# Moving conditioning blocks of an attention stage from TensorE to VectorE, GpSimd and ScalarE

## The chip, the cores and the metric

The kernel runs on one core of a Trainium2 chip. The metric is the device time of one execution in microseconds. The kernel before was run three times; the median is 1000.45 us. One further execution was recorded by the hardware profiler, and all profile lines come from it.

The core has five engines, each with a queue that it works through in order: TensorE (PE: matrix products and transposes), VectorE (DVE), ScalarE (ACT), GpSimd (POOL) and SyncE (SP, which here only issues DMA transfers). PEld is the loading of weights into TensorE, which overlaps its products.

## The reference

One step of a two-layer model over 128 context tokens and 256 latent tokens, with 1024 features. All arithmetic is float32. What matters here:

```python
def adaln(cond, w_ada, b_ada):                     # one conditioning vector per group
    mod = silu(cond) @ w_ada + b_ada               # 1024 -> 6 * 1024
    return split(mod, 6)                           # shift, scale, gate; twice
def modulate(h, shift, scale): return h * (1 + scale) + shift

for l in range(2):
    sm, cm, gm, sf, cf, gf = adaln(c, w_ada[l], b_ada[l])
    h = modulate(rmsnorm(x), sm, cm)
    mix = attention(h) if l == 0 else gmlp(h)
    x = x + gm * mix
    h = modulate(rmsnorm(x), sf, cf)
    x = x + gf * conv_ffn(h)
```

There are two conditionings, `c_ctx` for the context tokens and `c` for the latent tokens, so every modulation vector is computed for two input vectors with the same weights. In attention (layer 0) the latent queries see a window of their 4 x 64 grid, with a learned bias per head and offset, and 128 cached context keys in the same softmax; the context tokens attend to each other. There are 16 heads of 64 features.

## The kernel before, in words

Features lie on the 128 partitions and the 384 tokens on the columns. A weight is loaded as float32 into a tile `st`, rounded by ScalarE into `hi` and completed by VectorE with `lo = st - hi`; each product is then three products (`mac`, lines 112 to 114). These weight units (128 x 1024, 512 KB) come through a pool of three `st` tiles. In attention, `ready()` splits the oldest one and asks SP for another, `products()` uses one for the queries or the keys of one head pair.

The attention loop runs over eight head pairs. In a cycle of pair t, TensorE computes the scores of query block 0 (`scores(0)`, with those of the context queries), turns the first softmax of pair t-1 (`turn`), computes the products for the keys of t+1, the scores of query block 1, turns the second softmax of t-1, computes the products for the queries of t+1, and then the values of t-1 (`values`). On the other engines `exps` adds the bias (VectorE, line 636, with a minimum beside it) and takes exponentials with sums (ScalarE, line 646), `normalized` divides (VectorE, 651 and 653), `turned` copies the turned softmax from PSUM (ScalarE, 668 and 669; its result `pT` feeds `values`), `keys` and `queries` split into high and low parts (`khi`, `klo`, `qhi`, `qlo`). `bias(btr)` (line 619) writes the bias of the next pair into `bt`, from rows that SP has loaded into `btr` and a mask, by VectorE.

The conditioning is spread over the kernel in blocks of 512 KB. It is computed in two ways. `Ada` (lines 174 to 222) is TensorE's: a block is 128 rows of weights for 1024 outputs, four products of 128 x 256 with the two conditionings as stationary operand (line 199), accumulated over eight blocks; `flush` then turns the result with two transposes (line 215) and adds the bias (line 217). In attention it works off 16 blocks, of the second shift `SF` and the second scale `CF` of layer 0: two ahead of the loop and two at the end of each of the first seven cycles. `AdaV` (lines 226 to 271) is VectorE's: a block is the transposed weight of 128 outputs, `half(c, ...)` multiplies it with conditioning c, broadcast to all partitions (`cs[c]`), and sums over the columns in one instruction (line 260); after the second half the bias is added (line 263). In attention it works off eight blocks of the gate `GM`, one half after `exps(0)` and the other late in the cycle.

Blocks of `Ada` have a ring of two tiles (`adw`), blocks of `AdaV` in attention another of two (`adb`).

The program text is the order of work: for TensorE, ScalarE, VectorE and SP every instruction stands in its engine's queue in the order in which the code issues it. A load waits on SP until its tile is free, and all later loads wait behind it. GpSimd, in attention, only issues the output of the context keys (line 588) and of the values.

Of the kernel before, what the change touches and what calls it, by code (L numbers as in the profile page):

```python
# [11 lines left out]
AF = mybir.ActivationFunctionType  # L12
ALU = mybir.AluOpType
# [10 lines left out]
NPAIR = 8  # L24
# [6 lines left out]
SM, CM, GM, SF, CF, GF = range(6)  # L31
# [8 lines left out]
def backbone(ctx: ExitStack, tc: tile.TileContext, x_in, cond_in, condr_in, b_ada_in, prm_in,  # L40
# [17 lines left out]
    def bank(pool):  # L58
        return pool.tile([P, 512], F32, name="bank", tag="bank")
# [70 lines left out]

    def ada_tile(ring):

        tag = ("adw", "adb")[ring % 2]
        return adp.tile([P, D], F32, name=tag, tag=tag)

    def ada_load(f, late=False):

        w = []
        for hf in range(2):
            st = ada_tile(hf)  # L140
# [31 lines left out]
    class Ada:  # L172
# [3 lines left out]
        def __init__(self):  # L176
            order = [(0, SF), (0, CF)]
            self.todo = [(l, pc, k) for l, pc in order for k in range(KD)]
            self.ready = []
            self.pa = self.done = None  # L180

        def load(self, n):
            for _ in range(n):
                if len(self.ready) == ADA_BUFS or not self.todo:
                    return
                l, pc, k = self.todo.pop(0)
                t = ada_tile(0)
                nc.sync.dma_start(t, w_ada[k * P:(k + 1) * P, (pc - GM) * D:(pc - GM + 1) * D])
                self.ready.append((l, pc, k, t))
# [37 lines left out]
    class AdaV:  # L227


        def __init__(self):  # L230
            self.cs = self.junk = None

            def both(l, p, q):
                return [(l, pc, k) for k in range(KD) for pc in (p, q)]

            def one(l, p):
                return [(l, p, k) for k in range(KD)]

# [12 lines left out]

        def load(self, ring):
            l, pc, k = self.todo.pop(0)
            t = ada_tile(ring)
            nc.sync.dma_start(t, w_adaT[l, pc, k])
            return l, pc, k, t

        def half(self, c, l, pc, k, t):
            m = mods[l][:, pc, k]
            tc.keep_in_program_order(nc.vector.tensor_tensor_reduce(  # L260
                self.junk, t, self.cs[c], 1.0, 0.0, ALU.mult, ALU.add, m[:, c:c + 1]))
            if c:
                nc.vector.tensor_scalar(m, m, b_ada[:, l, pc * 8 + k:pc * 8 + k + 1], None, ALU.add)
                if pc in (CM, CF):
                    gain(l, pc, slice(k, k + 1))

        def run(self, n):
            for _ in range(n):
                block = self.load(len(self.todo))
                for c in range(2):  # L270
                    self.half(c, *block)
# [134 lines left out]
    def attention(pool, wkp):  # L406
# [208 lines left out]
        def bias(btr):  # L615
            for hh in range(2):
                v = btr[:, hh]
                slots = bass.AP(v.tensor, v.offset, [v.ap[0], (62, 3), (31, 2), (1, 64)])
                nc.vector.tensor_tensor(
                    bt[:, hh, 0::2].rearrange("p g (j c) -> p g j c", j=2),  # L620
# [90 lines left out]
        kT, btr = cache(1), bias_load(1)  # L711
        ada.run(2)
        ada.load(2)
        old = None
        for t in range(NPAIR):
# [5 lines left out]
            e = exps(0, sc, pr, pc)  # L721
            ada_v.half(0, *blocks[0])
            if old is not None:
# [41 lines left out]

        output(0, range(6), ps_mm)
        pT.append(turned(1, turn(*old[1])))
        normalized(*e)
# [5 lines left out]
        ready()  # L774
        ada_v.half(1, *blocks.pop(0))
        pT = [turned(0, turn(pr[0], pc[0]))]
# [263 lines left out]
```

## Time and profile before

| | us |
|---|---|
| median of three runs | 1000.45 (999.57 to 1000.53) |
| the profiled execution | 1000.85 |
| its span, first to last instruction | 998.0 |
| TensorE busy | 982.9 |
| VectorE busy | 797.4 |
| ScalarE busy | 476.3 |
| GpSimd busy | 15.8 |
| line 199 (conditioning on TensorE), busy | 8.6 |

Line 619 is the bias; line 260 the conditioning on VectorE. The loop's cycles begin at 67.2, 79.2, 95.4, 110.0, 124.9, 139.5, 154.2 and 168.8 us of the span; attention ends near 210. A line of a profile's group has the source line, the engine, the operation, output <- inputs, shapes, the count, busy time and mean duration of one in ns, and the idle time of that engine just before with what ended it. A line of the order of time has start and duration in us (of a merged run, where several instructions follow each other), engine and source line, the operation, and in brackets the idle time before it. A row of stretches has, for each engine, busy us and the number of instructions, then the granted TensorE clock, the DMA share and GB/s.

### The profile page before, as it was taken

The page shows a single profiled execution, that of the slowest core. Times are in us where ns is not written, and L with a number is a line of the kernel's source. Part 1 is how long each engine was busy: PE and PEld are TensorE (multiplying, and loading weights), DVE is VectorE, ACT ScalarE, POOL GpSimd, SP SyncE. Part 2 cuts the span into 40 slices and gives each one's busy share as a digit, 9 for nine tenths or more (in the row PEclk, how much of TensorE's full clock was granted, in tenths as well). Part 3 has the DMA queues.
Part 4 walks back from the last instruction along what each step waited for, and adds up shares of the span by engine and source line. Part 5 has one row for each costly group of instructions (what it writes and reads, how often), then busy time and mean ns, then how long its engine had stood idle before and what let it go on. Part 6 is the DMA issues. An engine that isn't in the chain of part 4 may idle for free.

```text
span 998.0 us, 15825 instructions
## 1 busy us (share of the span) xinstructions
PE 982.9 (98%) x5942; PEld 934.9 (94%) x5942; DVE 797.4 (80%) x1652; ACT 476.3 (48%) x846; POOL 15.8 (2%) x31
## 2 busy tenths in 40 slices
PE   8999999999999999999999999999999999999996
PEld 5788888899999999999988899999999999999996
DVE  5668888689998889899899999687698777777552
ACT  4455656558554544333363334333485444443331
POOL 1000000000000000000000000000000000000000
PEclk9999999999999999999999999999999999999999
DMA  9886676442464445677737756465235333435521
GB/s 338 313 292 179 206 233 201 138 148 85 148 190 152 167 148 156 201 220 220 235 105 256 251 174 185 149 204 177 84 106 182 122 126 121 127 114 180 161 72 63
DMA packets 53019, 172.94 MB, mean 173 GB/s; under 512 B 6016, under 2 KB 11152, under 8 KB 52944
## 3 DMA queue, kind: packets, MB, share of 16 engines
q1 hardware_dynamic: 51840, 169.33, 53.2%
q10 hardware_dynamic: 576, 1.31, 0.3%
q0 software_dynamic: 528, 1.32, 0.3%
q8 instruction: 46, 0.75, 0.3%
q14 instruction: 29, 0.24, 0.1%
HBM read 169.31 MB, written 2.62 MB: 172 GB/s over the span
## 4 chain that ended last, share of the span: by engine, by line
PE 94%; DVE 2%; ACT 1%; issue 1%; POOL 1%; DMA 1%; POOLq 0%; SPq 0%; ACTq 0%
PE bank L113 29%; PE bank L114 29%; PE bank L112 29%; PE bank L678 1%; PE bank L629 1%; PE bank L912 1%; PE bank L661 1%; PE bank L155 1%; PE bank L199 1%; POOL ry L331 1%; DMA lo<-in_x 1%; PE bank L322 0%; DVE lo L118 0%; PE bank L303 0%; DVE bank L636 0%
## 5 line engine op out<-in xcount | busy, mean ns | idle before, releaser
L113 PE MATMUL bank<-hlo,hi 128*128 128x384 f32 (+1 forms) x976 | 330.5, 339 | 0.1
L112 PE MATMUL bank<-hhi,hi 128*128 128x384 f32 (+1 forms) x976 | 330.1, 338 | 0.0
L114 PE MATMUL bank<-hhi,lo 128*128 128x384 f32 (+1 forms) x976 | 329.9, 338 | 0.2 <-DVE lo L118 0.2
L105 ACT CAST hi<-st 128x1024 fp32r<-128x1024 f32 (+1 forms) x184 | 189.1, 1030 | 295.3 <-PE bank L113 237.9
L106 DVE TENSOR_TENSOR lo<-st,hi 128x1024 fp32r<-128x1024 f32 (+1 forms) x184 | 220.5, 1198 | 62.5 <-ACT hi L105 62.3
L114 PEld LDWEIGHTS bank<-hhi,lo 128*128 128x128 f32 x976 | 184.1, 189 | 0.7 <-DVE lo L118 0.5
L112 PEld LDWEIGHTS bank<-hhi,hi 128*128 128x128 f32 x976 | 184.0, 189 | 0.8 <-ACT hi L105 0.4
L113 PEld LDWEIGHTS bank<-hlo,hi 128*128 128x128 f32 x976 | 183.4, 188 | 0.6 <-DVE hlo L118 0.3
L114 PE MATMUL bank<-ahi,lo 128*128 128x384 f32 x352 | 118.3, 336 | 0.0
L113 PE MATMUL bank<-alo,hi 128*128 128x384 f32 x352 | 118.3, 336 | 0.0
L112 PE MATMUL bank<-ahi,hi 128*128 128x384 f32 x352 | 118.1, 336 | 0.0
L260 DVE CUSTOM_DVE_ANT_0 junk<-adb,cs 128x1024 bf16<-128x1024 f32 x72 | 87.8, 1219 | 0.5
L260 DVE CUSTOM_DVE_ANT_0 junk<-adw,cs 128x1024 bf16<-128x1024 f32 x56 | 68.3, 1220 | 0.5
L114 PEld LDWEIGHTS bank<-ahi,lo 128*128 128x128 f32 x352 | 66.2, 188 | 0.0
L113 PEld LDWEIGHTS bank<-alo,hi 128*128 128x128 f32 x352 | 66.2, 188 | 0.0
L112 PEld LDWEIGHTS bank<-ahi,hi 128*128 128x128 f32 x352 | 66.2, 188 | 0.0
L112 PE MATMUL bank<-hi,hhi 128*128 128x512 f32 x144 | 58.1, 404 | 0.4 <-ACT hhi L453 0.4
L113 PE MATMUL bank<-lo,hhi 128*128 128x512 f32 x144 | 56.9, 395 | 0.1
L114 PE MATMUL bank<-hi,hlo 128*128 128x512 f32 x144 | 56.7, 394 | 0.0
L394 DVE SCALAR_TENSOR_TENSOR x<-bank,mod,x 128x128 f32<-128x128 f32 x64 | 23.8, 413 | 33.1 <-PE bank L114 33.0
L113 PE MATMUL bank<-mlo,hi 128*128 128x384 f32 x128 | 43.6, 341 | 0.0
L112 PE MATMUL bank<-mhi,hi 128*128 128x384 f32 x128 | 43.3, 338 | 0.0
(180 smaller groups left out, 1299.8 us busy)
## 6 DMA issues: line engine op xcount, KB each, us to landing
st<-in_w_up SPq DMA_DIRECT2D x88, 512.0 KB, 3.6
adb<-in_w_adaT SPq DMA_DIRECT2D x36, 512.0 KB, 4.5
st<-in_w_down SPq DMA_DIRECT2D x32, 512.0 KB, 3.6
adw<-in_w_adaT SPq DMA_DIRECT2D x28, 512.0 KB, 3.6
adw<-in_w_ada SPq DMA_DIRECT2D x24, 512.0 KB, 5.8
st<-in_w_qk SPq DMA_DIRECT2D x16, 512.0 KB, 4.2
st<-in_w_gu SPq DMA_DIRECT2D x16, 512.0 KB, 4.4
st<-in_w_gv SPq DMA_DIRECT2D x16, 512.0 KB, 4.4
```

Of the source, the lines that this page charges most:

```text
L105: nc.scalar.copy(hi[:, :n], st[:, :n])
L106: nc.vector.tensor_tensor(lo[:, :n], st[:, :n], hi[:, :n].bitcast(F32), ALU.subtract)
L112: nc.tensor.matmul(out, a[0], b[0], start=start, stop=False)
L113: nc.tensor.matmul(out, a[0], b[1], start=False, stop=False)
L114: nc.tensor.matmul(out, a[1], b[0], start=False, stop=stop)
L155: nc.tensor.matmul(pa[32 * j:32 * j + 32, 0:P], cond_s[:, 4 * hf + kk, :], w[hf][:, kk, P * q:P * q + P], start=(kk == 0), stop=(kk == 3), ...
L199: nc.tensor.matmul(self.pa[32 * j:32 * j + 32, 0:256], cond_s[:, k, :], t[:, 256 * j:256 * j + 256], start=(k == 0), stop=(k == KD - 1), t ...
L260: tc.keep_in_program_order(nc.vector.tensor_tensor_reduce(self.junk, t, self.cs[c], 1.0, 0.0, ALU.mult, ALU.add, m[:, c:c + 1]))
L331: nc.gpsimd.tensor_tensor(y, v, mhalf[:, :n], ALU.pow)
L394: nc.vector.scalar_tensor_tensor(x[m][:, a:b], ps[:, a:b], mod(l, gate, m, c), x[m][:, a:b], ALU.mult, ALU.add)
L629: nc.tensor.matmul(sc[hh][:, cols], q[qp][HS[hh], qs:qs + P], k[kp][HS[hh], ks], start=i == 0, stop=i == 2)
L661: nc.tensor.transpose((ta[:, o:o + P] if g < 2 else tb[:, o - 512:o - 512 + P]), pr[:, b, g * P:g * P + P], ident)
```

## The change

- `Ada` in attention does only the second scale `CF`: eight blocks, one ahead of the loop, one at the end of each of seven cycles and one behind the loop.
- `AdaV` does the gate `GM` and the shift `SF`, alternating: 16 blocks in attention, two in each cycle (A and B). For all but the last block, VectorE takes conditioning 0 as before (`half(0, ...)`), GpSimd multiplies the block in place with conditioning 1 (`shared`), ScalarE sums the product with a copy that has an accumulator (`summed`), and VectorE adds the bias (`biased`). A's sum stands behind the second `exps` of its cycle, B's in the next cycle, behind the split of a weight unit. The last block's two halves stay with VectorE, behind the loop.
- `bias(btr)` is computed by GpSimd.
- All blocks share one ring of four tiles (`adw` and `adb` in turn).
- In the first cycle the queries are split ahead of the next weight unit, in the others behind it.

```diff
-    def ada_tile(ring):
-        tag = ("adw", "adb")[ring % 2]
+    ada_count = iter(range(1 << 20))
+    def ada_tile():
+        tag = ("adw", "adb")[next(ada_count) % 2]
...
-            order = [(0, SF), (0, CF)]
+            order = [(0, CF)]
...
-            self.todo = (one(0, GM) + both(1, SM, CM)[:8]
+            self.todo = (both(0, GM, SF) + both(1, SM, CM)[:8]
...
             if c:
-                nc.vector.tensor_scalar(m, m, b_ada[:, l, pc * 8 + k:pc * 8 + k + 1], None, ALU.add)
-                if pc in (CM, CF):
-                    gain(l, pc, slice(k, k + 1))
+                self.biased(l, pc, k)
+
+        def biased(self, l, pc, k):
+            m = mods[l][:, pc, k]
+            nc.vector.tensor_scalar(m, m, b_ada[:, l, pc * 8 + k:pc * 8 + k + 1], None, ALU.add)
+            if pc in (CM, CF):
+                gain(l, pc, slice(k, k + 1))
+
+        def shared(self, l, pc, k, t):
+            self.half(0, l, pc, k, t)
+            nc.gpsimd.tensor_tensor(t, t, self.cs[1], ALU.mult)
+
+        def summed(self, l, pc, k, t):
+            nc.scalar.activation(t, t, AF.Copy, accum_out=mods[l][:, pc, k, 1:2])
...
-                nc.vector.tensor_tensor(
+                nc.gpsimd.tensor_tensor(
                     bt[:, hh, 0::2].rearrange("p g (j c) -> p g j c", j=2),
...
-        ada.load(2)
-        blocks = [ada_v.load(1) for _ in range(2)]
+        A, B = ada_v.load(), ada_v.load()
+        ada.load(1)
+        A2 = ada_v.load()
...
-        ada.run(2)
-        ada.load(2)
-        old = None
+        old = B1 = None
         for t in range(NPAIR):
...
             e = exps(0, sc, pr, pc)
-            ada_v.half(0, *blocks[0])
+            ada_v.shared(*A)
...
             ready()
+            if B1 is not None:
+                ada_v.summed(*B1)
+                ada.load(1)
+                if not last:
+                    A2 = ada_v.load()
...
             e = exps(1, sc, pr, pc)
+            ada_v.summed(*A)
             if last:
                 break
             if old is not None:
                 pT.append(turned(1, turn(*old[1])))
             bias(btr)
+            ada_v.shared(*B)
             normalized(*e)
-            ada_v.half(1, *blocks.pop(0))
+            if B1 is not None:
+                ada_v.biased(*B1[:3])
+            ada_v.biased(*A[:3])
+            B2 = ada_v.load()
             p = products()
-            ready()
-            Q = queries(p)
+            if old is not None:
+                ready()
+                Q = queries(p)
+            else:
+                Q = queries(p)
+                ready()
...
-            ada.run(2)
-            ada.load(2)
-            if t < NPAIR - 2:
-                blocks.append(ada_v.load(1))
+            ada.run(1)
+            A, B1, B = A2, B, B2
...
         output(0, range(6), ps_mm)
+        ada.run(1)
...
-        ada_v.half(1, *blocks.pop(0))
+        for blk in (B1, A):
+            ada_v.biased(*blk[:3])
+        for c in range(2):
+            ada_v.half(c, *B)
```

More of the change, by code (lines that the diff above doesn't have):

```diff
@@ L139, in ada_load @@
         for hf in range(2):
-            st = ada_tile(hf)
+            st = ada_tile()
             if late:
@@ L186, in load @@
                 l, pc, k = self.todo.pop(0)
-                t = ada_tile(0)
+                t = ada_tile()
                 nc.sync.dma_start(t, w_ada[k * P:(k + 1) * P, (pc - GM) * D:(pc - GM + 1) * D])
@@ L250, in silu, with load @@
                 nc.scalar.activation(self.cs[c], self.cs[c], AF.Silu)
-        def load(self, ring):
+        def load(self):
             l, pc, k = self.todo.pop(0)
-            t = ada_tile(ring)
+            t = ada_tile()
             nc.sync.dma_start(t, w_adaT[l, pc, k])
@@ L262, in half @@
             if c:
-                nc.vector.tensor_scalar(m, m, b_ada[:, l, pc * 8 + k:pc * 8 + k + 1], None, ALU.add)
-                if pc in (CM, CF):
-                    gain(l, pc, slice(k, k + 1))
+                self.biased(l, pc, k)
[9 more added lines that the diff above has]
+            nc.scalar.activation(t, t, AF.Copy, accum_out=mods[l][:, pc, k, 1:2])
         def run(self, n):
             for _ in range(n):
-                block = self.load(len(self.todo))
+                block = self.load()
                 for c in range(2):
```

## The prediction

> **What bounds the kernel now.** I read the page's busy shares and chain first, then the stretch of one cycle of the attention loop (one head pair, from the scores of query block 0 to those of the next pair), then that cycle in order of time on each engine.
>
> ```profile
> span 998.0 us, 15825 instructions
> PE 982.9 (98%) x5942; PEld 934.9 (94%) x5942; DVE 797.4 (80%) x1652; ACT 476.3 (48%) x846; POOL 15.8 (2%) x31
> PE 94%; DVE 2%; ACT 1%; issue 1%; POOL 1%; DMA 1%; POOLq 0%; SPq 0%; ACTq 0%
> 95.40:110.00 14.60, 14.60 (x116) 12.62 (x112) 12.13 (x33) 8.64 (x24) 0.54 (x1) 1.00 0.67 205
> ```
>
> TensorE is busy 98% of the span and for all 14.60 us of a cycle; VectorE is busy 12.13 of them, ScalarE 8.64, GpSimd 0.54. So what leaves TensorE here is worth its time, as long as the other engines go on delivering. How late they may be stands in the order of time. TensorE:
>
> ```profile
> 109.04 1.07 PE L199 MATMUL bank<-adw,cond_s 128*32 128x256 f32 x16
> 110.04 0.44 PE L629 MATMUL bank<-khi,qhi 64*128 64x384 f32 x2
> 121.91 0.38 PE L215 MATMUL bank<-ident,ada_sb 128*128 128x128 f32 x2
> 122.22 0.65 PE L678 MATMUL bank<-pT,V 128*64 128x256 f32 x4
> 154.15 0.44 PE L629 MATMUL bank<-khi,qhi 64*128 64x384 f32 x2
> 169.24 0.34 PE L629 MATMUL bank<-khi,qlo 64*128 64x384 f32 x2
> ```
>
> Two conditioning blocks (L199) hold TensorE from 109.04 to 110.04: 0.50 us a block. Without the two transposes of a finished chunk (L215, once), the values (L678) would have begun at 121.91. The first scores that read qlo come 15.09 us after the cycle's start (154.15 to 169.24); for the cycle from 110.04 that is 125.13. VectorE and ScalarE in that cycle:
>
> ```profile
> 112.55 1.21 DVE L260 CUSTOM_DVE_ANT_0 junk<-adb,cs 128x1024 bf16<-128x1024 f32 x1
> 114.64 0.75 DVE L653 TENSOR_SCALAR pr<-pr,st 128x384 f32<-128x384 f32 x2
> 115.31 0.47 DVE L653 TENSOR_SCALAR pc<-pc,st 128x128 f32<-128x128 f32 x2
> 116.23 1.23 DVE L118 TENSOR_TENSOR lo<-st,hi 128x1024 fp32r<-128x1024 f32 x1 [0.45 <-ACT hi L117]
> 118.53 0.56 DVE L636 CUSTOM_DVE_ANT_0 bank<-bank,bt 128x384 f32<-128x384 f32 x1
> 119.18 0.58 ACT L646 ACTIVATE pr<-bank,st 128x384 f32<-128x384 f32 x1 [0.27 <-DVE st L636]
> 119.52 1.02 DVE L619 TENSOR_TENSOR bt<-mask,btr 128x384 f32<-128x384 f32 x2
> 120.31 0.59 ACT L668 COPY pT<-bank 128x512 f32<-128x512 f32 x1
> 120.65 0.75 DVE L653 TENSOR_SCALAR pr<-pr,st 128x384 f32<-128x384 f32 x2
> 120.77 0.51 ACT L669 COPY pT<-bank 128x384 f32<-128x384 f32 x1
> 121.14 1.08 ACT L117 CAST hi<-st 128x1024 fp32r<-128x1024 f32 x1
> 121.32 1.22 DVE L260 CUSTOM_DVE_ANT_0 junk<-adb,cs 128x1024 bf16<-128x1024 f32 x1
> 122.58 0.23 DVE L263 TENSOR_SCALAR mod<-mod,b_ada 128x2 f32<-128x2 f32 x1
> 122.72 1.22 DVE L118 TENSOR_TENSOR lo<-st,hi 128x1024 fp32r<-128x1024 f32 x1
> 123.85 0.55 DVE L595 SCALAR_TENSOR_TENSOR qlo<-bank,qhi 128x384 fp32r<-128x384 f32 x1
> ```
>
> The second pT is copied by 121.28 and wanted at 121.91: 0.63 us of slack. qlo is done at 124.40 and wanted at 125.13: 0.73 us. Both slacks are short, and everything that the change adds to ScalarE and GpSimd stands ahead of these two.
>
> **The change, part by part.**
>
> *TensorE.* Eight of 16 blocks leave, and the two transposes of one chunk. Each of the seven cycles loses one block: 7 x 0.50 = 3.5 us at most. Of the last, one block is moved from ahead of the loop to behind it, which I count as nothing. The transposes were 0.31 us in front of the values, and the cycle with them is about 0.2 longer: -0.2.
>
> *ScalarE.* Each cycle gets two sums over 128x1024 with an accumulator. The nearest row is the square of x with the same shape and accumulator:
>
> ```profile
> 7.19 1.06 ACT L477 ACTIVATE hi<-lo 128x1024 f32<-128x1024 f32 x1 [0.47 <-DMA lo<-in_x]
> 8.25 0.20 ACT L481 ACTIVATE cond_s<-cond 128x16 f32<-128x16 f32 x1
> ```
>
> From one start to the next is 1.06 us. The old B's sum stands behind the first cast of a weight unit and before the keys; ScalarE has gaps there (it waits at 119.18), and by the order of the casts I estimate that exps(1) moves by 0.2. A's sum stands between exps(1) and the pT copies, with no gap: the copies, the next cast, its lo and qlo all move by 1.06.
>
> *VectorE.* Per cycle it still has two reductions of 1.2 us (the other conditioning's half moves to another block, not away); it loses the bias subtraction (1.02) and gains one 0.23 addition. That is a gain of 0.8 in busy time, but lo then waits for ScalarE's cast, not for VectorE.
>
> *GpSimd.* It gets a 128x1024 product of two SBUF tiles twice a cycle and two 128x384 subtractions. No row shows such an instruction. The nearest, and a clash:
>
> ```profile
> 3.63 0.32 POOL masks.py:199 TENSOR_SCALAR_AFFINE_SELECT ident<-ident 128x128 f32<-128x128 f32 x1
> 9.80 0.24 DVE L334 SCALAR_TENSOR_TENSOR rt<-rt,rv 128x3 f32<-128x3 f32 x1
> 9.81 0.53 POOL L415 TENSOR_SCALAR_AFFINE_SELECT mask<-mask 64x48 f32<-64x48 f32 x2
> 10.08 0.16 DVE L336 SCALAR_TENSOR_TENSOR rr<-rt,ry 128x3 f32<-128x3 f32 x1
> 219.32 1.23 DVE L106 TENSOR_TENSOR lo<-st,hi 128x1024 fp32r<-128x1024 f32 x1
> 219.56 1.74 POOL L331 TENSOR_TENSOR ry<-rv,mhalf 128x3 f32<-128x3 f32 x1 [55.70 <-DVE rv L329]
> 495.58 0.85 POOL L331 TENSOR_TENSOR ry<-rv,mhalf 128x3 f32<-128x3 f32 x1 [274.29 <-DVE rv L329]
> ```
>
> A select over 128 columns takes 0.32, one over 48 about 0.24 (0.53 for two, lapping): 1.1 ns a column and 0.18 fixed, with one operand read. If a second operand costs nothing, the product is 0.18 + 1024 x 1.1 ns = 1.3 us and a subtraction 0.6; if it costs as much as the first, 2.4 and 1.0. I take the upper ends, because the product has two full operands to fetch. [...]
>
> GpSimd's 128x3 power takes 0.85 at 495.58, with VectorE idle, and 1.74 at 219.56, under VectorE's lo, which ends at 220.55: it looks as if it began only then. In the other direction, L334, which has tiny operands, took 0.24 beside the first select where its like L336 took 0.16. So the two engines block each other, and I let whoever asks first hold the other off to its end. [...]
>
> Through one cycle, with lo, the reductions and the normalization (whose 384 columns cost only 0.14 more than 128: 0.47 and 0.75 for two) exposed:
> - Reduction of A ends at 113.8. GpSimd's product holds 113.9 to 116.3. Normalization, due at 114.64 and 1.14 long, runs 116.3 to 117.4; lo starts at 117.4, not 116.23. exps(1) is 1.2 late: VectorE is done with it at 120.8, ScalarE at 121.5.
> - ScalarE: sum 1.06, copies 0.97, cast 1.0: pT at 123.5, the cast at 124.5. TensorE begins the values at 123.6, 1.7 later than 121.91.
> - VectorE: reduction of B 120.8 to 122.0; GpSimd's first subtraction, which asked in between, to 123.0; normalization to 123.8; second subtraction to 124.8; lo 124.8 to 126.0; qlo to 126.5. The qlo scores start at 126.6, against 125.13: **+1.47 us**. (By TensorE's own line, 123.6 + 1.67 + 0.5 + 0.45 = 126.2.)
> - B's product, asked for at 124.8, comes behind lo, at 126.0, and ends before A's next reduction.
>
> Six cycles have this shape (pairs 1 to 6): 6 x 1.47 = +8.8. Pair 0 has no copies of pT, and its queries are moved ahead of a lo:
>
> ```profile
> 81.10 0.45 PE L629 MATMUL bank<-khi,qlo 64*128 64x384 f32 x2 [1.27 <-DVE qlo L595]
> 176.26 0.45 PE L114 MATMUL bank<-ohi,lo 128*128 128x384 f32 x1 [0.27 <-DVE lo L118]
> ```
>
> That can give back the 1.27 wait, and the two blockings (1.2 and up to 2.4) can take it: between -1.3 and +1.2, taken as 0. In pair 7 TensorE already waits for lo at 176.26; a product ahead of normalization makes that 1.1 longer. The two extra half reductions behind the loop lie under the output projection.
>
> **Sum:** 8.8 - 0.2 + 0 + 1.1 = +9.7 us. The profiled execution took 1000.85 (span 998.0, 2.85 around it), 0.4 over the median 1000.45 of the runs: 1010.5 by its own time, 1010 as a median.
>
> *Queues.* SP waits in its queue for the sums before it reloads a slot:
>
> ```profile
> adw<-in_w_ada SPq DMA_DIRECT2D x14, 512.0 KB, 6.0
> 117.49 6.81 SPq L558 DMA_DIRECT2D st<-in_w_qk  x2
> ```
>
> The loads stay three blocks and two weight units a cycle. But TensorE's block is now asked for behind the unit at 117.49, not a cycle ahead, and lands 6.0 later, at 123.5 or more, in a cycle that wants it about 125.3 as forecast. Behind it on SP stand A's next block, then B's, the next unit and the bias rows, none wanted within 9 us.
>
> **The rivals.**
>
> 1. *GpSimd wins the second race.* B's product asks at 124.8 and lo at 124.5; if the product goes first (a cast 0.3 later would do), it holds VectorE from 124.8 to 127.2, lo ends at 128.4 and qlo at 128.9: +3.87 a cycle, 6 x 3.87 + 0.9 = +24, **1024.5**. For it: 0.3 us decides. Against it: lo does ask first in the sum.
> 2. *ScalarE cancels TensorE's gain.* The product takes 1.3, or VectorE passes GpSimd: then normalization is no later than its own slack, exps(1) moves by 0.2 and the pT copies by 1.26. Values at 122.6, TensorE's scores 0.09 later than before, qlo 0.17 later. 6 x 0.17 - 0.2 - 1.3 (pair 0) = -0.5: **1000**. For it: GpSimd's price is only bounded. Against it: the 1.74.
> 3. *TensorE stays the bound.* If pT and qlo keep up, the 3.5, the 0.2 and pair 0's 1.3 are all gained: -5.0, **995.5**. For it: 14.60 of 14.60 busy, and VectorE has 0.8 less to do. It decides where A's sum takes under 0.6 of the copies' time, as if ScalarE had run it in a gap. Against it: 1.06 us in the queue ahead of copies with 0.63 slack.
> 4. *The ring.* Without blocking, TensorE would want its block at 123.4, and 117.49 + 6.0 is past that, more so with three loads in a row (up to 1 us): 7 x 1 on top of rival 2, **1007**.
>
> **How the numbers follow.** Forecast 0.36, rival 1 0.14, rival 2 0.20, rival 3 0.24, rival 4 0.06. The likeliest gives 1010; its own range, with GpSimd's product from 2.0 to 2.6 and a race lost in one or two cycles, is 1006 to 1016. The whole range must reach into rivals 3 and 1: 996 to 1024 leaves out about half of each, 0.2. A difference of 0.2% (2 us) is what a measurement of this kernel can tell from none. Slower: 0.36 + 0.14 + 0.06 and 0.04 of rival 2, 0.60. Faster: 0.24 and 0.04 of rival 2, 0.28. Same: 0.12.
>
> **What would show it.** TensorE's L199 has half its matmuls, and a cycle's stretch is 16 us with TensorE idle about 2 of it, waiting for qlo (VectorE) and pT (ScalarE). The means of L653 and of lo rise, because the blocked time shows in their duration, as in the 1.74; GpSimd's product shows 2.4 or more. ScalarE's sums show 1.06. It is wrong if L653 stays at 0.4 beside running products (rival 2 or 3), if the cycle is 14.1 with TensorE full (rival 3), if it is 18 (rival 1), or if L199 waits for a DMA (rival 4).

## The result and the profile after

The kernel after the change takes 1037.38 us (median of four runs, 1036.98 to 1038.29); the kernel before, run beside it, takes 1000.37 (999.57 to 1000.53). The ratio is 1.0371, with a 95% interval of 1.0359 to 1.0383: 37 us slower, where 10 were forecast and 996 to 1024 was the range. The profiled execution took 1038.29, with a span of 1036.5 against 998.0, so 38.5 us are to be explained.

The page of the kernel after: the span, each engine's busy time, the granted TensorE clock in 40 slices, and the shares of the chain that ended last.

```profile
span 1036.5 us, 15808 instructions
PE 996.9 (96%) x5875; PEld 946.2 (91%) x5876; DVE 831.6 (80%) x1645; ACT 492.2 (47%) x875; POOL 67.2 (6%) x62
PEclk9999898889999999999999999999999999999999
PE 82%; DVE 9%; issue 4%; ACT 3%; DMA 2%; POOL 1%; POOLq 0%; ACTq 0%; SPq 0%; DVEq 0%
```

TensorE has 67 matmuls fewer and is busy 14 us more: in attention (58 to 220 us of the span) it was granted a clock of 0.91 on average, where it had 1.00. The chain has passed 12 points from TensorE to the others, 7 of them to VectorE. Where the time lies is told by the stretches from one pair's first scores to the next pair's (after; length, then busy time of PE, PEld, DVE, ACT and POOL, clock, DMA share, GB/s):

```profile
67.49:82.49 15.00, 13.23 (x75) 11.31 (x76) 13.01 (x26) 7.96 (x22) 5.69 (x5) 0.89 0.43 115
82.49:100.12 17.63, 15.14 (x105) 12.50 (x105) 16.57 (x30) 11.59 (x29) 7.66 (x6) 1.00 0.52 166
137.25:155.26 18.01, 15.15 (x108) 12.49 (x105) 16.48 (x32) 10.74 (x29) 6.89 (x6) 1.00 0.47 157
155.26:174.14 18.88, 16.07 (x108) 13.90 (x105) 17.36 (x32) 10.82 (x29) 7.77 (x6) 0.91 0.52 171
```

A full cycle that took 14.6 takes 17.6 to 19.7, counted from first scores to first scores. The seven cycles take 126.34 us (67.49 to 193.83) and took 101.57 (67.22 to 168.79): +24.8, of which pair 0 has 3.0 and the other six 21.8. What lies behind the loop takes 842.7 and took 829.2: +13.5. Ahead of it are +0.3. In a cycle VectorE is now busy 16.5 of 18.0 us, where it was busy 12.1 of 14.6, though it lost the bias. The groups between 58 and 225 us show why (after; count, then busy, mean ns of one, idle before):

```profile
L668 DVE TENSOR_SCALAR pr<-pr,st 128x384 f32<-128x384 f32 x32 | 38.6, 1245 | 0.6
L262 DVE CUSTOM_DVE_ANT_0 junk<-adb,cs 128x1024 bf16<-128x1024 f32 x8 | 17.7, 2207 | 0.0
```

and the same two of the kernel before:

```profile
L260 DVE CUSTOM_DVE_ANT_0 junk<-adb,cs 128x1024 bf16<-128x1024 f32 x16 | 19.5, 1216 | 0.0
L653 DVE TENSOR_SCALAR pr<-pr,st 128x384 f32<-128x384 f32 x32 | 12.0, 417 | 0.6
```

Normalization costs 1245 ns an instruction instead of 417, and half of the reductions of this group take 3.2 us instead of 1.22. On GpSimd stand the instructions that run at those moments (after):

```profile
L276 POOL TENSOR_TENSOR adb<-adb,cs 128x1024 f32<-128x1024 f32 x8 | 19.1, 2384 | 28.2 <-DVE mod L262 17.4 <-PE bank L644 6.1 <-DVE st L666 3.5
L634 POOL TENSOR_TENSOR bt<-mask,btr 128x384 f32<-128x384 f32 x16 | 15.3, 979 | 47.8 <-DMA btr<-in_rpb 47.7
```

One cycle in order of time, first VectorE, from the reduction of A to the lo that stands ahead of qlo (after; start, duration):

```profile
142.67 1.22 DVE L262 CUSTOM_DVE_ANT_0 junk<-adw,cs 128x1024 bf16<-128x1024 f32 x1
...
144.77 2.21 DVE L668 TENSOR_SCALAR pr<-pr,st 128x384 f32<-128x384 f32 x2
...
149.58 0.56 DVE L651 CUSTOM_DVE_ANT_0 bank<-bank,bt 128x384 f32<-128x384 f32 x1
...
150.57 3.21 DVE L262 CUSTOM_DVE_ANT_0 junk<-adb,cs 128x1024 bf16<-128x1024 f32 x1
...
153.71 0.15 DVE L666 RECIPROCAL st<-st 128x2 f32<-128x2 f32 x1
153.90 2.87 DVE L668 TENSOR_SCALAR pr<-pr,st 128x384 f32<-128x384 f32 x2
...
156.96 1.21 DVE L118 TENSOR_TENSOR lo<-st,hi 128x1024 fp32r<-128x1024 f32 x1
```

GpSimd in the same stretch (after):

```profile
144.03 2.40 POOL L276 TENSOR_TENSOR adw<-adw,cs 128x1024 f32<-128x1024 f32 x1 [6.09 <-DVE mod L262]
...
150.87 1.82 POOL L634 TENSOR_TENSOR bt<-mask,btr 128x384 f32<-128x384 f32 x2
153.87 2.36 POOL L276 TENSOR_TENSOR adb<-adb,cs 128x1024 f32<-128x1024 f32 x1 [1.18 <-DVE st L666]
```

(The last bracket names the reciprocal, which ended last; the product itself only needs the reduction of B.) A's product ends at 146.43, and the normalization that began beside it ends at 146.98: 2.21 us instead of 0.75. Both subtractions run to 152.69, and the reduction of B ends at 153.78, 1.09 later: about its own 1.22. B's product ends at 156.23, the normalization at 156.77. Each time VectorE's row lasts through GpSimd's remaining time and then for its own, less 0.1 to 0.2: 0.55 and 0.54 for two normalizations that take 0.75 alone. TensorE sees the sum of it (after; the wait is in the bracket):

```profile
76.24 0.44 PE L114 MATMUL bank<-hhi,lo 128*128 128x384 f32 x1 [1.76 <-DVE lo L118]
...
118.95 0.44 PE L644 MATMUL bank<-khi,qhi 64*128 64x384 f32 x2
...
121.82 0.47 PE L644 MATMUL bank<-khi,qlo 64*128 64x384 f32 x2 [2.26 <-DVE qlo L610]
...
140.40 0.44 PE L644 MATMUL bank<-khi,qlo 64*128 64x384 f32 x2 [2.53 <-DVE qlo L610]
...
209.22 1.08 PE L201 MATMUL bank<-adb,cond_s 128*32 128x256 f32 x8 [5.67 <-DMA adb<-in_w_ada]
```

Over the attention part TensorE's waits by what ended them are (us in total, times, longest):

```profile
PE bank L644 <- DVE qlo L610: 16.6, 7, 2.8
PE bank L201 <- DMA adb<-in_w_ada: 5.7, 1, 5.7
PE bank L114 <- DVE lo L118: 2.5, 3, 1.8
```

There is no wait for pT among the large ones. The second row is the one behind the loop: the eighth block of `CF`, whose products TensorE wants at 203.5. SP's queue says when it was asked for (after; waiting in the queue counts as duration):

```profile
195.83 8.94 SPq L573 DMA_DIRECT2D st<-in_w_o  x2
204.87 0.38 SPq L190 DMA_DIRECT2D adb<-in_w_ada  x1
```

The load of that block stands behind two weight units of the output projection, and the second of these waits until VectorE has split an earlier unit (lo from 203.21 to 204.43) and its tile is free. So the block was asked for at 204.87 and landed at 209.2.

Last, the clock. After the wait that ended at 121.82, in stretches of the kernel after (the number before the DMA share):

```profile
118.95:121.70 2.75, 0.61 (x8) 0.29 (x4) 2.75 (x7) 0.02 (x1) 0.41 (x1) 1.00 0.12 48
121.70:123.00 1.30, 1.18 (x9) 1.06 (x10) 0.56 (x3) 0.00 (x0) 0.00 (x0) 0.65 0.40 44
123.00:124.00 1.00, 1.00 (x6) 1.00 (x6) 1.00 (x5) 0.00 (x0) 0.00 (x0) 0.50 0.88 361
...
125.00:126.00 1.00, 1.00 (x6) 1.00 (x5) 0.59 (x2) 1.00 (x5) 0.28 (x1) 0.74 0.45 103
```

After this wait TensorE is granted half its speed (0.50) for about 3.5 us. So it is with seven of its nine waits of 1.76 us and more, but not with those of 2.05 and 2.53 us that ended at 85.15 and 140.40, after which the clock stayed at 1.00. Around the waits that ended at 176.97 and 209.22 it was 0.50 for 6.8 us, from 176.7 and from 207.4 on. That follows the waits and can add to them.

### The profile page after: what moved, and what is told of

The parts are those of the page before. It is cut to its first block, busy times and chain, and to the rows that moved or that the text cites. A ratio compares the mean times of both kernels' runs of the same rounds, so it can differ in the third digit from the quotient of the medians.

```text
span 1036.5 us, 15808 instructions
## 1 busy us (share of the span) xinstructions
PE 996.9 (96%) x5875; PEld 946.2 (91%) x5876; DVE 831.6 (80%) x1645; ACT 492.2 (47%) x875; POOL 67.2 (6%) x62
## 4 chain that ended last, share of the span: by engine, by line
PE 82%; DVE 9%; issue 4%; ACT 3%; DMA 2%; POOL 1%; POOLq 0%; ACTq 0%; SPq 0%; DVEq 0%
PE bank L113 26%; PE bank L114 26%; PE bank L112 26%; DVE junk L262 2%; DVE lo L118 2%; PE bank L945 1%; DVE bank L651 1%; DMA st<-in_w_up 1%; PE bank L157 1%; ACT pr L661 1%; DVE pr L668 1%; PE bank L644 1%; DVE klo L118 1%; POOL ry L346 1%; ACT pc L661 0%
## 5 line engine op out<-in xcount | busy, mean ns | idle before, releaser
L114 PEld LDWEIGHTS bank<-hhi,lo 128*128 128x128 f32 x976 | 186.2, 191 | 3.7 <-DVE lo L118 3.5
L112 PEld LDWEIGHTS bank<-hhi,hi 128*128 128x128 f32 x976 | 186.4, 191 | 2.4 <-ACT hi L105 2.0
L113 PEld LDWEIGHTS bank<-hlo,hi 128*128 128x128 f32 x976 | 185.6, 190 | 0.6 <-DVE hlo L118 0.3
L262 DVE CUSTOM_DVE_ANT_0 junk<-adw,cs 128x1024 bf16<-128x1024 f32 x65 | 85.2, 1311 | 0.5
L346 POOL TENSOR_TENSOR ry<-rv,mhalf 128x3 f32<-128x3 f32 x6 | 7.0, 1162 | 824.7 <-DVE rv L344 824.7
```

The source lines that it names most:

```text
L112: nc.tensor.matmul(out, a[0], b[0], start=start, stop=False)
L113: nc.tensor.matmul(out, a[0], b[1], start=False, stop=False)
L114: nc.tensor.matmul(out, a[1], b[0], start=False, stop=stop)
L262: tc.keep_in_program_order(nc.vector.tensor_tensor_reduce(self.junk, t, self.cs[c], 1.0, 0.0, ALU.mult, ALU.add, m[:, c:c + 1]))
L346: nc.gpsimd.tensor_tensor(y, v, mhalf[:, :n], ALU.pow)
```

## The experiments

Three explanations stood against each other: that an instruction of GpSimd holds one of VectorE off to its end (theory L in the expectations), that the lower clock after the waits costs most of it (theory C), and that the order of loads and ScalarE's sums do (theory S). The first four kernels take out one or two suspects each.

**The bias back to VectorE.**

```diff
-                nc.gpsimd.tensor_tensor(
+                nc.vector.tensor_tensor(
                     bt[:, hh, 0::2].rearrange("p g (j c) -> p g j c", j=2),
```

> The changed kernel with the bias subtraction back on VectorE; the products stay on GpSimd. [...] A cycle goes from 18.0 to about 17.0; with fewer slow-clock stretches 1027 us, between 1022 and 1031. Theory S (ScalarE's sums in front of the pT copies and SP's waits for them make the cycle long, and the long durations on VectorE are harmless): no gain, 1037 or 1 us a cycle worse.

Measured: 1027.88 against 1001.67, ratio 1.0267 [1.0235, 1.0298]; 9.5 us less than the kernel after, close to the 1027 that theory L gives. The groups of this kernel:

```profile
L668 DVE TENSOR_SCALAR pr<-pr,st 128x384 f32<-128x384 f32 x32 | 38.7, 1250 | 0.6
L262 DVE CUSTOM_DVE_ANT_0 junk<-adb,cs 128x1024 bf16<-128x1024 f32 x8 | 9.7, 1215 | 0.0
```

The reduction of B is back at 1.22, the normalization stays at 1250 ns. So the subtractions held the reduction, and the products hold the normalization. The seven cycles take 117.3 us, 9.0 less, though VectorE has taken back 1.0 us of work in each.

**No products on GpSimd.**

```diff
         def shared(self, l, pc, k, t):
             self.half(0, l, pc, k, t)
-            nc.gpsimd.tensor_tensor(t, t, self.cs[1], ALU.mult)
```

> The changed kernel without GpSimd's products: left out is the multiplication with conditioning 1 for 15 of the 16 blocks in attention, so that ScalarE sums the bare block. The sums, the ring and the bias on GpSimd stay. Theory L: both normalizations go back to 0.75 us for two; the reduction of B still waits for the two subtractions (3.2 us); qlo comes some 0.3 us later than in the kernel before, a cycle is about 14.8 us; 1003 us, between 998 and 1008. Theory S: the sums are all there, so the time stays above 1030.

Measured: 1013.83, 1.0126 [1.0084, 1.0169]; 23.5 us less than after. The mean of the normalization falls to 453 ns, and the group with the reduction of B stays at 2192. The expectation of 1003 left out the late block: here too TensorE waits 6.3 us for it, and that, with what comes behind it, is most of the difference; a cycle also takes 15.4 us and not 14.8. In this kernel one of the races goes the other way. VectorE in three of its cycles:

```profile
121.06 3.17 DVE L262 CUSTOM_DVE_ANT_0 junk<-adw,cs 128x1024 bf16<-128x1024 f32 x1
...
136.43 3.17 DVE L262 CUSTOM_DVE_ANT_0 junk<-adb,cs 128x1024 bf16<-128x1024 f32 x1
...
151.80 1.22 DVE L262 CUSTOM_DVE_ANT_0 junk<-adw,cs 128x1024 bf16<-128x1024 f32 x1
```

and GpSimd in the same three:

```profile
121.32 1.81 POOL L633 TENSOR_TENSOR bt<-mask,btr 128x384 f32<-128x384 f32 x2
...
136.70 1.81 POOL L633 TENSOR_TENSOR bt<-mask,btr 128x384 f32<-128x384 f32 x2
...
152.06 2.74 POOL L633 TENSOR_TENSOR bt<-mask,btr 128x384 f32<-128x384 f32 x2
```

In the first two GpSimd goes first and the reduction takes 3.17; in the third the reduction goes first and the subtractions take 2.74. Either of the two can be held. The subtraction's row begins 0.26, 0.27 and 0.26 us behind the reduction's, so with the same 0.26 it went both ways, and in the first cycle of the loop GpSimd went first at 0.24 (76.06 and 76.30). The reduction's row begins together with the reading of the accumulator of the instruction ahead of it (0.14 us, in the third cycle from 151.80 as the reduction itself). When the reduction wants its operands the rows don't show, and what decides the race can't be read from them.

**Neither products nor bias on GpSimd** (both edits).

> As the run without products, and the bias on VectorE as well, so GpSimd does nothing in the loop but issue DMAs; left out is the same multiplication. ScalarE's sums, the loads' order and TensorE's smaller work stay. Theory L: this is rival 2 of the prediction, ScalarE's delay against TensorE's gain: 14.6 us a cycle, 1000 us, between 996 and 1004. Theory S: above 1030.

Measured: 1009.22, 1.0080 [1.0049, 1.0111]. The seven cycles take 101.32 us, against 101.57 of the kernel before, and a full cycle 14.82 against 14.63. So all that the loop lost comes from GpSimd's instructions, and without them it gains almost nothing either. The expected 1000 is missed behind the loop, by the block that comes late:

```profile
180.95 1.08 PE L201 MATMUL bank<-adb,cond_s 128*32 128x256 f32 x8 [6.21 <-DMA adb<-in_w_ada]
```

**Matmuls that keep TensorE busy.** Eight products of constants stand ahead of the first scores of each cycle, and twenty ahead of the last block; they fill waits and change no result.

```diff
+            if t:
+                busy(8, sc[0])
             scores(0, Q, K, sc)
...
         output(0, range(6), ps_mm)
+        pv = bank(ps_sc)
+        busy(20, pv)
         ada.run(1)
```

> The changed kernel with idle-time matmuls on TensorE: eight 128x512 bf16 products into the score bank ahead of each scores(0) but the first (about 1.7 us, in a wait of 1.9 to 2.8 us), and twenty ahead of the last conditioning block behind the loop (about 4.3 us, in a wait of 5.7 us). Nothing else changes; VectorE is blocked as before. Theory C (the waits cost twice: after one of them the granted clock is 0.5 for some 3.4 us): the clock stays at 1.0 in the loop, TensorE's real products lose no time, cycles are all near 18.0; 8 to 14 us less than the changed kernel, 1023 to 1029. If the slow clock has another cause (the load of the other engines, a timer), it stays at 0.98 over the span, and the time stays at 1037 or rises.

Measured: 1033.33, 1.0321 [1.0278, 1.0364]; 4 us less than after, where 8 to 14 were expected. One cycle of this kernel, with the clock ahead of the DMA share:

```profile
101.29:119.60 18.31, 17.03 (x115) 13.29 (x114) 16.73 (x32) 10.71 (x28) 7.16 (x5) 1.00 0.52 164
```

The clock stays at 1.00 in the loop, but for 3.4 us in pair 0, which has no added products, and from pair 2 on every cycle takes 18.3. So the waits do cause the lower clock. But the seven cycles take 125.84 us, only 0.5 less than in the kernel after. There too it is 18.3 to 18.6 us from one cycle's scores with qlo to the next one's, with a drop of the clock or without, and 19.4 once, where the clock was low for over 6 us: VectorE is the bound, and most of the slow matmuls lie beside it. The profiled executions differ by 6.2 us, of which 5.1 lie behind the loop, around the wait for the late block. The lower clock was a small part, and of the loop's loss hardly any.

**The last block asked for earlier**, at the end of pair 6, into the tile whose products have just been made:

```diff
             if B1 is not None:
                 ada_v.summed(*B1)
-                ada.load(1)
                 if not last:
+                    ada.load(1)
                     A2 = ada_v.load()
...
             ada.run(1)
+            if t == NPAIR - 2:
+                next(ada_count)
+                ada.load(1)
```

> The changed kernel, but the last conditioning block of TensorE is asked for at the end of pair 6's cycle, into the tile of the block just used, and not in pair 7 behind the sum of B. Theory: the 5.7 us in which TensorE waits for this block behind the loop go, and with them the slow clock that follows (0.5 for about 3.4 us, worth 1.7); some wait for lo or pT may take up to 2 of it; 1031 us, between 1029 and 1034. If the wait only uncovers another one as long, 1037.

Measured: 1030.93 against 999.98, 1.0309 [1.0290, 1.0327]; 6.5 us less than after, as expected. TensorE no longer waits for a load, and what lies behind the loop is 5.8 us longer than before the change, not 13.5.

**Products over half the columns** (512 of 1024; the other half is summed as it is).

```diff
-            nc.gpsimd.tensor_tensor(t, t, self.cs[1], ALU.mult)
+            nc.gpsimd.tensor_tensor(t[:, :512], t[:, :512], self.cs[1][:, :512], ALU.mult)
```

> The changed kernel with each GpSimd product over 512 of the 1024 columns; left out is the multiplication of the other half. Theory L: a product takes about 1.3 us; normalization behind A's product, due 0.8 us after it starts, loses some 0.35 instead of 1.46, that behind B's 1.0 instead of 2.1; a cycle drops by about 2.2 us to 15.8; with fewer slow-clock stretches 1013 us, between 1006 and 1022. [...]

Measured: 1024.49, 1.0244 [1.0225, 1.0263], 2.5 us outside the range of theory L. The groups of this kernel on GpSimd and VectorE:

```profile
L276 POOL TENSOR_TENSOR adb<-adb,cs 128x512 f32<-128x512 f32 x8 | 10.2, 1277 | 28.5 <-DVE mod L262 23.7 <-DVE st L666 3.5 <-PE bank L201 1.2
```

```profile
L668 DVE TENSOR_SCALAR pr<-pr,st 128x384 f32<-128x384 f32 x32 | 22.1, 730 | 0.6
```

1277 ns for 512 columns and 2384 for 1024 give 2.16 ns a column and 0.17 us fixed. Half the product's time gives 13 of the 23.5 us that the whole product costs: the loss follows the length of the instruction. The total alone would also fit a VectorE that is only slowed while both run. Against that stand the rows: B's product, from 128.82, ends at 130.10, and the two normalizations beside it, from 128.85, end at 130.64, again 0.54 us behind GpSimd's end as with the whole product. Had both gone on at a lower speed, what was left to do would have depended on how long both had run.

**The kernel before with the queries of pair 0 ahead of the weight unit.**

```diff
             p = products()
-            ready()
-            Q = queries(p)
+            if old is not None:
+                ready()
+                Q = queries(p)
+            else:
+                Q = queries(p)
+                ready()
```

> The kernel before with one edit of the change alone: in pair 0 the queries are split ahead of the next weight unit. TensorE's wait of 1.27 us for qlo in front of pair 1 goes: 999.0 us, between 998.6 and 999.6; if the moved lo then makes exps(0) late and the wait comes back there, 1000.4.

Measured: 999.60 against 999.98, 0.9992 [0.9983, 1.0001]: by this time it can't be told from no change. The spans, without what lies around them, are steadier and show the gain: the median of the eleven runs is 996.7, that of the fifteen runs of the kernel before 997.9. In the profile TensorE's wait of 1.27 us for qlo is gone, and the stretch that had it, from pair 1's first scores to pair 2's, takes 15.05 instead of 16.20. So the edit gives back about 1.2 us, as expected.

**No work on GpSimd, and the last block in time** (the third and the fifth kernel together).

> The run without GpSimd's products and bias, and with the last conditioning block asked for in pair 6; left out is the multiplication with conditioning 1 for 15 of the 16 blocks. What remains of the change is TensorE's smaller work, ScalarE's 15 sums, the ring and the order of the first queries. Theory: without the wait of 6.2 us for the last block and the slow clock behind it, this is the second rival of the prediction in full, -0.5 us against the kernel before: 1000, between 998 and 1001.5. If the tail's loss has another cause, 1006 or more.

Measured: 1002.45 against 1000.48, 1.0026 [1.0016, 1.0037], 1 us outside the range. The cycle is 14.82 again. What is left, 2.0 us, lies behind the loop: that part is 2.9 longer in the profiled execution, with TensorE waiting 1.2 for a `hi` and 0.8 for a pT. Which of the moved instructions does that was not separated. In the loop, the lo ahead of qlo now waits for ScalarE's cast, which stands behind A's sum:

```profile
138.88 1.23 DVE L118 TENSOR_TENSOR lo<-st,hi 128x1024 fp32r<-128x1024 f32 x1 [0.47 <-ACT hi L117]
```

**Dodging.** These four ask whether the work can be shared with GpSimd at all. In each, VectorE does both halves of A and computes the bias itself in two parts, the last block is asked for early, and only B is multiplied by GpSimd. In the first the product is held back by a tiny GpSimd instruction that reads `lo`, so that it starts behind VectorE's split of the weight unit; in the second it isn't.

```diff
             e = exps(0, sc, pr, pc)
-            ada_v.shared(*A)
+            ada_v.half(0, *A)
+            if not last:
+                bias(btr, 0)
...
-            bias(btr)
-            ada_v.shared(*B)
+            ada_v.half(1, *A)
             normalized(*e)
+            ada_v.half(0, *B)
...
+            tc.keep_in_program_order(nc.gpsimd.tensor_tensor(gt, units[-1][1][:, 0, 0:4].bitcast(F32), mhalf, ALU.mult))
+            tc.keep_in_program_order(nc.gpsimd.tensor_tensor(B[3], B[3], ada_v.cs[1], ALU.mult))
```

> [...] The shift's block (B) goes half to GpSimd, half to VectorE, and GpSimd's product is held back by a tiny operation on the lo of the second weight unit, so it runs under qlo, olo and exps(0), which read PSUM. The gate's block (A) goes to VectorE alone, as in the kernel before. The bias, split by query block into two tiles, is written by VectorE in its gaps, so that the longer second half of the cycle is paid by the bias that left it. One sum per cycle on ScalarE. The last block of TensorE is asked for in pair 6. Theory L: no normalization or lo is held off (pr at 0.42 us); a cycle loses TensorE's 0.5 us and gets perhaps 0.1 of it back as a wait for qlo; 7 x 0.4 + 1.3 = 4 us less than before: 996, between 994.5 and 998.5. If GpSimd disturbs VectorE's PSUM operations too, or TensorE, above 1001.

> The same, but without the operation that holds the product back: GpSimd multiplies as soon as VectorE has reduced B, ahead of lo, so only the place of the same product differs. Theory L: lo is held off by about 2 us in each of seven cycles (it is due some 0.3 us after the product starts), qlo and the scores wait: 14 us more than the version with the product held back, and more where the clock drops: 1010, between 1006 and 1018. If what counts is that GpSimd works at all, both take the same.

Measured: 1013.11, 1.0123 [1.0107, 1.0140], and 1014.76, 1.0143 [1.0123, 1.0163], against 1000.48. Both miss. The normalization isn't held in the first (418 ns), but the bias, moved to an earlier place, now waits for its rows:

```profile
120.89 0.76 DVE L636 TENSOR_TENSOR bt<-mask,btr 128x256 f32<-128x256 f32 x2 [1.45 <-DMA btr<-in_rpb]
```

So the pair was repeated with the rows loaded most of a cycle ahead.

```diff
+            if t < NPAIR - 2:
+                btr2 = bias_load(t + 2)
...
-                kT, btr = cache(t + 2), bias_load(t + 2)
+                kT, btr = cache(t + 2), btr2
```

> The version with the held-back product, but the bias rows of each pair are asked for most of a cycle earlier, since in the last version VectorE waited 1.45 us a cycle for their transfer ahead of normalization and lo. Theory L: normalization, lo and the reductions keep their own durations, the cycle is 14.1 to 14.4 us, 996 between 994.5 and 999. [...]

> The same with the earlier bias rows, and the product not held back: it runs as soon as VectorE has reduced B, ahead of lo. Theory L: the one difference is that lo is held off, by some 2 us a cycle, of which 1.5 or more reach qlo and the scores: 10 to 16 us above the version with the product held back. If what counts is that GpSimd works at all, both take the same.

Measured: 1003.10, 1.0028 [1.0018, 1.0039], and 1003.66, 1.0032 [1.0020, 1.0045], against 1000.22. The first is the best that the experiments found for sharing the work, and it is still 0.3% slower than before. That loss does not lie in the loop's later cycles, which take 14.6 us as before: the seven together take 0.4 more, and what lies behind the loop 3.1 more, much as in the version without GpSimd. A cycle on VectorE has two gaps to speak of (0.35 and 0.33), and GpSimd's product lies beside instructions that it doesn't hold:

```profile
111.00 2.38 POOL L787 TENSOR_TENSOR adb<-adb,cs 128x1024 f32<-128x1024 f32 x1
```

```profile
111.96 0.57 DVE L653 CUSTOM_DVE_ANT_0 bank<-bank,bt 128x384 f32<-128x384 f32 x1 [0.35 <-PE bank L646]
...
119.31 0.29 DVE L118 TENSOR_TENSOR klo<-bank,khi 128x128 fp32r<-128x128 f32 x1 [0.33 <-ACT khi L117]
```

VectorE is full for all but 0.7 to 0.8 us of a cycle of 14.6. The half microsecond that TensorE no longer needs isn't gained, and the likely reason is that VectorE is the next bound just behind it. The second kernel was expected 10 to 16 us above the first and came out level. Its VectorE and GpSimd:

```profile
111.31 0.22 DVE L269 TENSOR_SCALAR mod<-mod,b_ada 128x2 f32<-128x2 f32 x1
111.44 1.22 DVE L118 TENSOR_TENSOR lo<-st,hi 128x1024 fp32r<-128x1024 f32 x1
```

```profile
111.53 3.35 POOL L776 TENSOR_TENSOR adb<-adb,cs 128x1024 f32<-128x1024 f32 x1 [3.36 <-DVE mod L269]
```

Here VectorE goes on without a gap to lo, lo keeps its 1.22, and the product is held for the microsecond: 3.35 instead of 2.38. It lands where the held-back product lands. In the kernel after, a reciprocal of 0.15 us stood between the reduction that frees the block (to 153.78) and the normalization; GpSimd began at 153.87 and the normalization at 153.90, and there GpSimd went first. That the reciprocal made the difference is read from the times; no kernel leaves it out.

## Why the prediction was wrong, step by step

**The prices were right.** A product took 2.384 us (2.4 in the sum), a subtraction 0.979 (1.0), ScalarE's sum 1.05. The upper ends were the right ones.

**The blocking was right, and so was what it does at A.** The prediction read one 1.74 us row as mutual blocking with no example of a long GpSimd instruction holding VectorE. That a hold lasts to the end of an instruction, and that lo, the reductions and the normalization are open to it, was the author's assumption in the sum; no run of before shows it. The runs after the change have the example in every cycle (a reduction at 3.2 us instead of 1.22, normalizations at 1245 ns instead of 417; beside lo six of seven products waited in the last kernel, 3.35 instead of 2.38, and all its lo together took 2.1 us more than with the product held back), the blocked time does stand in the duration of the blocked instruction, and it goes when GpSimd's part is taken out (417 ns without, 453 with the bias alone, 1250 with the products alone). At A: from the scores with qlo to `exps(1)` it was 8.04 us (110.49 to 118.53) and is 9.18 (140.40 to 149.58), +1.14, where 1.2 was forecast. ScalarE's second pT copy is done 12.96 us after those scores and was done 10.79 after them: +2.17, where the sum had 2.2:

```profile
151.36 1.05 ACT L280 ACTIVATE adw<-adw 128x1024 f32<-128x1024 f32 x1
...
152.87 0.49 ACT L684 COPY pT<-bank 128x384 f32<-128x384 f32 x1
```

TensorE waited little for that pT, though, where the forecast had the values begin 1.7 later for it: they begin 12.22 us behind the scores with qlo, 0.8 later than they could have begun before (121.91 less 110.49 is 11.42), and the one wait for pT that the trace shows among them, of a weight load, is 0.22.

**The first step that failed is the order at B.** The sum had "VectorE: reduction of B 120.8 to 122.0; GpSimd's first subtraction, which asked in between", then normalization, the second subtraction, lo, and "B's product, asked for at 124.8, comes behind lo". Measured is: both subtractions, reduction, product, normalization, lo. Both subtractions lie ahead of lo in the sum too, so they cost lo nothing more. But as they passed the reduction together, GpSimd was free when B was reduced, and the product was asked for at the same moment as the normalization and not behind it. It went first: lo starts 16.56 us after the scores with qlo, where the sum had 14.3 (124.8 less 110.49), and the 2.3 between them is about one product (2.36). A cycle costs 3.4 us more and not 1.47. That is close to the first rival's 3.87, which had a chance of 0.14; it too put the product ahead of lo, by a race with lo itself. The prediction's own sign for it, a cycle of 18, came true. The six cycles cost 21.8 against 8.8.

That one engine holds the other off to its end was not what failed. Whether the first to ask goes first stays partly open. GpSimd's product waited where it was asked for 0.09 behind lo, and went first where it was 0.03 ahead of the normalization; that fits. The rows with 0.26 don't settle it. What failed is that the times of asking were worked out to tenths from a schedule that the change itself shifts, and one outcome was put into the sum for all six cycles. Where the end of one reduction frees both engines, the sum should have carried both outcomes as equals; the price of the lost race, one product, stood in the sum.

**Pair 0** was taken as 0, between -1.3 and +1.2, and is +3.0. It has the same two lost races as the others (a reduction of 3.19 at 78.26). The 1.27 us that the moved queries were to give back are real, as the kernel before with that edit alone shows, but the wait stood behind pair 1's first scores, and in the kernel after TensorE waits 2.05 there (at 85.15): the races took the gain and more.

**What lies behind the loop** was taken as +1.1 and is +13.5. The paragraph on queues followed the loads through a cycle and found none wanted within 9 us. It did not follow them past the end of the loop, where the block that had been moved "from ahead of the loop to behind it, which I count as nothing" is asked for behind two weight units. (The kernel works off seven blocks of `CF` in the cycles and the eighth behind the loop; ahead of the loop one is only loaded, though the list of the change counts it there as well.) With the load in time, 6.5 us of the time go; of the 5.8 that then stay behind the loop, 2.9 stay without GpSimd's work too. The late load has nothing to do with the engines that the change is about.

**The lower clock** after a wait was in no term. By the kernel with filled waits it is worth about 4 us of the time, most of it behind the loop, around the late block; the seven cycles became 0.5 us shorter.

**The rivals.** Rival 2, no blocking, was run in effect by taking GpSimd's work out: +0.19 us a cycle, where +0.17 had been worked out, and by its mechanism: the late cast makes lo and qlo late. Rival 3, TensorE remaining the bound, doesn't come true even then: its 0.5 us a cycle isn't gained. In that kernel with the last block in time (cycle from 125.81 to 140.63, against 125.34 to 139.98 before), TensorE's conditioning block takes 0.57 us and not 1.00; but the scores with qlo start 0.83 behind the first scores and not 0.46, and the values begin 0.11 later and take 0.13 longer. That makes up the 0.18. Rival 4's late block was looked for in the cycles and stood behind them.

Taken apart by runs, one after another: 23.5 us go with the products (1037.38 to 1013.83), 4.6 more with the bias (1009.22), 6.8 more with the load in time (1002.45), and 2.0 remain. The order matters: the bias alone, with the products still there, is worth 9.5. The kernels ran at different times, with the kernel before between 999.98 and 1001.67 beside them, so these shares are good to about 1 us.

## What to carry to other kernels

Before work moves from VectorE or TensorE to GpSimd, list the instructions of VectorE that can run at the same time and price each overlap as a race that VectorE loses, from the length of the GpSimd instruction; the busy share of GpSimd, 6% of the span here, says nothing about that: its products alone cost 23.5 us. Look at what the second busiest engine has left: with the sharing at its best, VectorE had 0.7 us of gaps left in a cycle of 14.6, and TensorE's 0.5 us was not gained. Idle time alone is no promise either: without GpSimd's work VectorE was busy 12.5 of 14.8 us, and qlo was late all the same, behind ScalarE's cast. And follow a load that a change moves to the point where it is wanted, past the end of the loop too, through everything that its queue must wait for.

## What the runs showed of the hardware

- **In these kernels VectorE and GpSimd held each other off to the end of an instruction, in both directions.** A 128x384 normalization takes 1245 ns on average instead of 417, a two-operand reduction 3.2 us instead of 1.22, and a product on GpSimd 3.35 instead of 2.38 when VectorE was first. `exps`, which reads one operand from PSUM, was not held: 0.57 beside the product in the first of the repeated kernels. Two GpSimd instructions that follow each other directly both went ahead of a waiting VectorE instruction (1.82 us at 150.87).
- **Who goes first can't be told from the rows when both ask within a quarter of a microsecond.** With a subtraction's row 0.24 to 0.27 behind the reduction's, GpSimd went first in six cycles and VectorE in one, and at 0.26 it went both ways. A product 0.03 ahead of the normalization went first, behind a reciprocal of 0.15 us; one 0.09 behind lo waited.
- **A wait shorter than the drop that it causes.** After waits of TensorE of 1.76, 2.26 and 2.81 us the granted clock was 0.50 for about 3.5 us; after those of 2.05 and 2.53 us it stayed at 1.00. So the length of a wait does not decide it alone. Nor does TensorE's busy time just before: in the 2.75 us up to 121.70, ahead of a drop, it was 0.61, and in the 3.15 us up to 140.40, with no drop behind them, 0.62.
